# A planned order for one hybrid attention and mLSTM layer: ties between ready steps go to the earliest latest-beginning, taken from a rehearsal of the plan

## The chip, the cores and the metric

The kernel runs on one core of a Trainium2 chip. The metric is device time in microseconds (us) for one execution, the median of several. Engines are named as in the profile: PE (TensorE: matmuls; PEld its weight loads), DVE (VectorE), ACT (ScalarE), POOL (GpSimd) and SP (SyncE, which issues nearly all DMAs here). SPq, ACTq and the like are the queues that issue DMAs.

## What is computed

One encoder layer over 2048 tokens of width 1024, all in float32:

```
xn = rms_norm(x, mix_norm_g)
proj = xn @ w_in                       # q, k, v | mq, mk, mv, mo, i, f | ga, gm
att = chunk_band_attention(aq, ak, av, rel_bias)      # 8 heads of 64, own chunk + 8 before
mqk = silu(causal_depthwise_conv([mq, mk], conv_w, conv_b))
hm = rms_norm(mlstm_chunkwise(mq_c, mk_c, mv, ipre + b_igate, fpre + b_fgate))   # 4 heads of 128
y = sigmoid(ga) * (att @ w_att_proj) + sigmoid(gm) * ((sigmoid(mo) * hm) @ w_mlstm_proj)
x = x + y @ w_out
x = x + square(relu(rms_norm(x, ffn_norm_g) @ w_up)) @ w_down      # 1024 -> 4096 -> 1024
out = rms_norm(x, final_norm_g)
```

## The kernel before

**Arithmetic.** Each float32 operand of a large product is split into a rounded high part and a rest (type fp32r): ACT casts the high part, DVE subtracts to get the rest. A product of two tiles is then three matmuls of 128x128 by 128x512 (high by high, high by rest, rest by high); `pe` steps of the large products hold three such matmuls. The large products use Strassen's scheme with seven sub-products per 2x2 of blocks (`quad`, `product`, `down`): sums of activation blocks (L1765 for the input and output operands, L1855 to L1864 for the up projection's) and of weight blocks (L520, or L438 through DRAM) come ahead of the split, and the products are added into their places by DVE (L1798, L780, L755, L2183) behind it.

**Tiles.** A weight tile of 128x1024 lands in one of 4 `wraw` buffers, is split by L501 (ACT, high) and L503 (DVE, rest) into one of 3 `wsp` buffers, and feeds 24 matmuls. An activation tile of 128x512 is split into one of 28 `r` buffers by L1109 (ACT) and L1114 (DVE), with a scale by L1111 and L1116; `r<-u` are the hidden activations of the feed-forward, read back from DRAM. Products gather in 8 PSUM banks. `ctx`, `tmp` and `sc` are working buffers of 128x512 or somewhat more.

**Stages on PE, from the trace.** Two blocks of v and mv (L562 to L564), from 98 us the other input columns of the first half of the tokens (L631), from 455 us the input columns of the second half (L662 and L667) with the projections of token blocks 0 and 1, from 1097 us the out and up projections of the first half (L631), then its down projection (L562 to L564) with the projections of blocks 2 and 3 (`project`) up to about 2010 us, then out, up and down of the second half, and from 2678 us to 2725 us a last seventh product with tokens on the partitions (L856). Attention (L1337 scores, L1369 transposes of the probabilities, L1262 the weighted sum) and the mLSTM recurrence (L1586 to L1651) run between the large products from 463 to 1936 us. An attention head's result for block 2 goes straight into an operand of `project`: L1275, L1280 (DVE), L1285 (ACT, high part), L1287 (DVE, rest). At the end, for each of four token tiles, L2282 and L2286 (DVE) add and scale, L2298 (ACT) squares and sums, L2289 (DVE) and L2291 (POOL) make the factor, L2308 (ACT) or L2311 (DVE) applies it, and L2316 (ACTq) or L2319 (SPq) stores.

**What sets the order.** Nothing above is written out in its final order. Every piece of work is a generator (a thread) that yields steps: an engine and a modelled duration, or a wait for an event, or a request for buffers of a pool. `Flow.run` is the planner: it keeps a modelled clock per engine, and again and again takes, of all threads whose next step could run, the one with the smallest key

```
key = (start, prio, th.n)
```

where `start` is the later of the engine's clock and the moment that the step's inputs are there (by the model's latencies), `prio` is the thread's fixed priority (weights 0, most evacuations and splits 1, sums of weights 3, the dense products on PE 5; a `!` behind the engine's name puts -1), and `th.n` the order of creation. The step's instructions are then written, so the order of the plan becomes the order of each engine's instructions. Where several steps wait for a busy engine, all have the same `start` (the engine's clock), so `prio` and then `th.n` decide between them. On PE, steps of `prio` below 5 (attention, recurrence) are put off by `FAR` or `SLACK`, 1300 model ns. SP's steps are planned in the same way. A callback (`near`) ties each DVE instruction to those planned 10 us before it, and each ACT instruction to those 6 us before, so that the framework's own scheduler does not move them far.

## Time and profile before

| | |
|---|---|
| median of three runs, lowest, highest | 2738.43, 2737.99, 2741.09 us |
| the profiled execution's own time, its span | 2734.73, 2732.9 us |
| granted TensorE clock | 1.00 |
| busy: DVE, ACT, POOL | 2074.9 us (76%), 1527.6 us (56%), 48.2 us (2%) |
| matmul records, DVE and ACT instructions | 12832, 3685, 2650 |
| HBM, mean | 245 GB/s |
| 16 DMA engines, packets of SP's queue | 73.0% |

Busy times are of one execution, and the span is that of its first to last instruction. "Idle before" of an instruction is the time its engine stood still ahead of it, with the instruction that ended the wait behind an arrow.

### The profile page before, as it was taken

The page shows a single profiled execution, that of the slowest core. Times are in us where ns is not written, and L with a number is a line of the kernel's source. Part 1 is how long each engine was busy: PE and PEld are TensorE (multiplying, and loading weights), DVE is VectorE, ACT ScalarE, POOL GpSimd, SP SyncE. Part 2 cuts the span into 40 slices and gives each one's busy share as a digit, 9 for nine tenths or more (in the row PEclk, how much of TensorE's full clock was granted, in tenths as well). Part 3 has the DMA queues.
Part 4 walks back from the last instruction along what each step waited for, and adds up shares of the span by engine and source line. Part 5 has one row for each costly group of instructions (what it writes and reads, how often), then busy time and mean ns, then how long its engine had stood idle before and what let it go on. Part 6 is the DMA issues. An engine that isn't in the chain of part 4 may idle for free.

```text
span 2732.9 us, 38055 instructions
## 1 busy us (share of the span) xinstructions
PE 2717.4 (99%) x12832; PEld 2262.6 (83%) x12832; DVE 2074.9 (76%) x3685; ACT 1527.6 (56%) x2650; POOL 48.2 (2%) x79
## 2 busy tenths in 40 slices
PE   9999999999999999999999999999999999999998
PEld 8878888888888888888888888888888888888887
DVE  7868776788875778897767798879888665657675
ACT  6545446676742534566556776666445565554443
POOL 0000000000000000000000000000000000000000
PEclk9999999999999999999999999999999999999999
DMA  8877678888868889767768876877774454588863
GB/s 297 280 257 259 243 266 280 269 250 266 281 215 271 306 307 303 239 216 261 254 230 279 277 254 204 255 229 245 252 233 160 154 204 158 185 276 272 286 234 138
DMA packets 331240, 672.53 MB, mean 246 GB/s; under 512 B 36788, under 2 KB 66100, under 8 KB 331044
## 3 DMA queue, kind: packets, MB, share of 16 engines
q1 hardware_dynamic: 330324, 669.03, 73.0%
q8 instruction: 101, 1.65, 0.2%
q10 hardware_dynamic: 720, 1.06, 0.1%
q14 instruction: 95, 0.78, 0.1%
HBM read 458.27 MB, written 211.68 MB: 245 GB/s over the span
## 4 chain that ended last, share of the span: by engine, by line
PE 90%; DVE 6%; issue 1%; DMA 1%; ACT 1%; POOL 0%; SPq 0%; POOLq 0%; DVEq 0%; ACTq 0%
PE bank L631 37%; PE bank L662 11%; PE bank L562 9%; PE bank L563 9%; PE bank L564 9%; PE bank L667 3%; PE bank L1337 2%; PE bank L1262 2%; PE bank L1369 2%; PE bank L856 1%; DVE wsp L503 1%; DVE r L1114 1%; DMA x<-ctx 1%; PE bank L1420 1%; PE bank L1597 1%
## 5 line engine op out<-in xcount | busy, mean ns | idle before, releaser
L631 PE MATMUL bank<-r,wsp 128*128 128x512 f32 x4872 | 1110.6, 390 | 1.9 <-ACT r L1109 1.1
L631 PEld LDWEIGHTS bank<-r,wsp 128*128 128x128 f32 x4872 | 912.6, 188 | 194.9 <-ACT r L1109 1.8
L501 ACT CAST wsp<-wraw 128x1024 fp32r<-128x1024 f32 x439 | 461.3, 1051 | 540.9 <-PE bank L563 203.7
L503 DVE TENSOR_TENSOR wsp<-wraw,wsp 128x1024 fp32r<-128x1024 f32 x439 | 536.1, 1221 | 277.8 <-ACT wsp L501 271.8
L562 PE MATMUL bank<-r,wsp 128*128 128x512 f32 x1088 | 430.4, 396 | 0.0
L563 PE MATMUL bank<-r,wsp 128*128 128x512 f32 x1088 | 425.0, 391 | 1.6 <-DVE r L1287 1.6
L564 PE MATMUL bank<-r,wsp 128*128 128x512 f32 x1088 | 424.7, 390 | 0.0
L662 PE MATMUL bank<-r,wsp 128*128 128x512 f32 x1512 | 368.5, 393 | 1.3 <-DVE ctx L755 0.8
L662 PEld LDWEIGHTS bank<-r,wsp 128*128 128x128 f32 x1512 | 278.9, 188 | 58.3 <-DVE ctx L755 1.5
L564 PEld LDWEIGHTS bank<-r,wsp 128*128 128x128 f32 x1088 | 204.2, 188 | 43.6
L563 PEld LDWEIGHTS bank<-r,wsp 128*128 128x128 f32 x1088 | 204.6, 188 | 40.4 <-DVE r L1287 2.0
L562 PEld LDWEIGHTS bank<-r,wsp 128*128 128x128 f32 x1088 | 204.3, 188 | 38.5 <-DVE r L1374 0.3
L1114 DVE TENSOR_TENSOR r<-r 128x512 fp32r<-128x512 f32 x271 | 179.8, 688 | 16.1 <-ACT r L1109 13.4
L1109 ACT CAST r<-r 128x512 fp32r<-128x512 f32 x271 | 157.9, 617 | 31.0 <-DMA r<-u 27.6
L1798 DVE TENSOR_TENSOR ctx<-bank,ctx 128x512 f32<-128x512 f32 x150 | 103.0, 687 | 64.1 <-PE bank L631 64.0
L520 DVE TENSOR_TENSOR wraw<-wraw,wraw 128x1024 f32<-128x1024 f32 x112 | 136.2, 1219 | 3.8 <-DMA wsum<-wraw 2.8
L1350 ACT ACTIVATE sc<-sc,scs 128x640 f32<-128x640 f32 (+4 forms) x128 | 97.5, 762 | 67.1 <-DVE scs L1343 66.4
L2119 ACT ACTIVATE ctx<-ctx 128x512 f32<-128x512 f32 x96 | 60.5, 630 | 105.7 <-DVE ctx L1798 105.6
L1790 ACT COPY ctx<-bank 128x512 f32<-128x512 f32 x150 | 87.3, 582 | 53.4 <-PE bank L631 51.3
L1374 DVE TENSOR_TENSOR r<-bank,r 128x512 fp32r<-128x512 f32 (+1 forms) x168 | 95.6, 593 | 14.5 <-ACT r L1372 13.8
L1372 ACT CAST r<-bank 128x512 fp32r<-128x512 f32 (+1 forms) x168 | 80.9, 515 | 31.3 <-PE bank L1369 29.3
L1262 PE MATMUL bank<-r,r 128*128 128x512 f32 x336 | 95.2, 365 | 0.0
(257 smaller groups left out, 3060.6 us busy)
## 6 DMA issues: line engine op xcount, KB each, us to landing
wraw<-in_wf SPq DMA_DIRECT2D x196, 512.0 KB, 4.4
r<-u SPq DMA_DIRECT2D x224, 256.0 KB, 4.2
wraw<-wsum SPq DMA_DIRECT2D x104, 512.0 KB, 4.5
u<-ctx SPq DMA_DIRECT2D x128, 256.0 KB, 2.4
u<-tmp SPq DMA_DIRECT2D x96, 256.0 KB, 2.4
wraw<-in_w SPq DMA_DIRECT2D x47, 512.0 KB, 4.4
ctx<-in_wf SPq DMA_DIRECT2D x88, 256.0 KB, 3.9
wsum<-ctx SPq DMA_DIRECT2D x88, 256.0 KB, 3.4
```

The costliest lines, as they stand in the source:

```text
L501: nc.scalar.copy(w[:, 0], raw)
L503: nc.vector.tensor_sub(w[:, 1], raw, w[:, 0].bitcast(F32))
L520: V.tensor_sub(dst, x, y)
L562: mm(ps, lh, rh, start=first, stop=False)
L563: mm(ps, lh, rl, start=False, stop=False)
L564: mm(ps, ll, rh, start=False, stop=last)
L631: mm(ps, wv[:, x, k, n], a[:, y], start=new and k == 0 and x == y == 0, stop=k == 3 and x == 1, skip_group_check=True)
L662: mm(ps, wv[:, x, k, n], a[:, y], start=start and x == y == 0, stop=stop and x == 1, skip_group_check=True)
L1109: self.nc.scalar.copy(dst[:, 0], src)
L1114: self.nc.vector.tensor_sub(dst[:, 1], src, dst[:, 0].bitcast(F32))
L1262: nc.tensor.matmul(bkv[:, :, c0:c0 + w], st, sl[:, :, o:o + w], start=n == 0, stop=n == total - 1)
L1798: nc.vector.tensor_add(t[:, o:o + 512], ps, t[:, o:o + 512])
```

## The change

`kernel` now builds the layer twice. The first time (`Layer(Blank(), ...)`) every tile, DRAM tensor and engine call is a `Blank` that swallows what is done to it, so nothing is written; the planner runs by the old key and logs each step with its start, its end and the steps that it waited for (`th.by`, through events, buffer pools and the thread's own previous step). `dues` then goes through the log backwards and gives each step the latest beginning with which everything behind it would still begin in time; the only fixed points are the dense PE steps (`prio` 5), which must begin when they did in the rehearsal. Steps that lead to none of these get a very late time. The second build plans again, and on ACT, DVE, POOL and SP the second place of the key is now that latest beginning instead of `prio` (steps with `!` keep coming first). The first place of the key, the earliest start, is as before, and on PE the whole key is.

```diff
--- before.py
+++ after.py
@@ -69,14 +69,40 @@
 
 
 
+ENGS = ("act", "dve", "pool", "sp")
+PEDUE = lambda prio: prio == 5
+SPM = 0.0
+TRIES = 1
+
+
 class Event:
     def __init__(self):
         self.at = None
+        self.by = ()
+
+
+class Blank:
+
+
...
+    def tile(self, *a, **kw):
+        return Blank()
 
 
 class Pool:
     def __init__(self, items):
-        self.free = [((0.0, "sp"), n, i) for n, i in enumerate(items)]
+        self.free = [((0.0, "sp"), n, i, ()) for n, i in enumerate(items)]
         self.n = len(items)
 
 
@@ -94,9 +120,10 @@
 
 
 class Thread:
-    def __init__(self, gen, prio, n, at):
+    def __init__(self, gen, prio, n, at, name, by):
         self.gen, self.prio, self.n, self.at = gen, prio, n, at
         self.req = None
+        self.name, self.kids, self.steps, self.by = name, 0, 0, list(by)
 
 
 class Flow:
@@ -114,7 +141,9 @@
                dve=dict(pe=220.0, act=130.0, dve=130.0, pool=155.0), pool=dict(pe=290.0, act=130.0, dve=60.0),
                sp=dict())
 
-    def __init__(self):
+    def __init__(self, due=None):
+        self.due = due
+        self.log, self.cur = [], None
         self.now = (0.0, "sp")
         self.clock = dict(pe=0.0, act=0.0, dve=0.0, pool=0.0, sp=0.0)
         self.ready, self.blocked = [], []
@@ -122,17 +151,24 @@
         self.full = False
 
     def spawn(self, gen, prio=2):
-        th = Thread(gen, prio, self.count, self.now)
+        up = self.cur
+        if up is None:
+            th = Thread(gen, prio, self.count, self.now, f"{self.count}", ())
+        else:
+            th = Thread(gen, prio, self.count, self.now, f"{up.name}.{up.kids}", up.by)
+            up.kids += 1
         self.count += 1
         self._step(th, None)
 
     def set(self, ev):
         ev.at = self.now
+        ev.by = tuple(self.cur.by)
 
     def put(self, pool, *items, late=0.0):
 
         for i in items:
-            pool.free.append(((self.now[0] + late, self.now[1]), pool.n, i))
+            by = tuple((x, y + late) for x, y in self.cur.by) if self.cur else ()
+            pool.free.append(((self.now[0] + late, self.now[1]), pool.n, i, by))
             pool.n += 1
             if isinstance(pool, Banks):
                 pool.dense.discard(id(i))
@@ -143,6 +179,7 @@
             if any(e.at is None for e in r[1]):
                 return False, None
             th.at = max([th.at] + [e.at for e in r[1]])
+            th.by += [x for e in r[1] for x in e.by]
             return True, None
         pool, n = r[1], r[2]
         room = len(pool.free)
@@ -157,19 +194,21 @@
         pool.free.sort(key=lambda x: x[:2])
         got, pool.free = pool.free[:n], pool.free[n:]
         th.at = max([th.at] + [g[0] for g in got])
+        th.by += [x for g in got for x in g[3]]
         if kind == "dense":
             pool.dense.update(id(g[2]) for g in got)
         return True, [g[2] for g in got]
 
     def _step(self, th, value):
-        keep = self.now
+        keep, up = self.now, self.cur
         while True:
-            self.now = max(self.now, th.at)
+            self.now, self.cur = max(self.now, th.at), th
             try:
                 th.req = th.gen.send(value)
             except StopIteration:
-                self.now = keep
+                self.now, self.cur = keep, up
                 return
+            self.cur = up
             if th.req[0] in ("wait", "get", "dense"):
                 ok, value = self._grant(th)
                 if ok:
@@ -212,6 +251,8 @@
                     start = max(self.clock[e], start)
                     if e == "pe" and self.full and not full:
                         start += self.SWITCH
+                    if self.due is not None and e in ENGS:
+                        prio = -1e12 if prio < 0 else self.due.get((th.name, th.steps), 1e12)
                     key = (start, prio, th.n)
                     if best is None or key < best[0]:
                         best = (key, th, e, full)
@@ -223,10 +264,31 @@
             self.clock[e] = end
             if len(th.req) > 2:
                 end += th.req[2]
+            at = th.name, th.steps
+            self.log.append((at, e, start, end, th.prio, {x: y for x, y in sorted(th.by, key=lambda x: x[1])}))
+            th.steps += 1
+            th.by = [(at, 0.0)]
             th.at = self.now = (end, e)
             self._step(th, e)
 
 
+def dues(log):
+    late, of = {}, {x[0]: x[1:4] for x in log}
+    due = {}
+    for at, e, start, end, prio, by in reversed(log):
+        end_by = late.get(at, 1e12) - (SPM if e == "sp" else 0.0)
+        begin = end_by - (end - start)
+        if e == "pe" and PEDUE(prio):
+            begin = min(begin, start)
+        due[at] = begin
+        for x, wait in by.items():
+            lat = Flow.LAT[of[x][0]].get(e, 0.0) + wait
+            if e == "pe" and prio < 5:
+                lat += Flow.FAR
+            late[x] = min(late.get(x, 1e12), begin - lat)
+    return due
+
+
 def act_ns(n, ps=False, ap=0):
     return (51 if ps else 93) + 0.834 * n + 93 * ap
 
@@ -248,9 +310,9 @@
 class Layer:
     LATE, LANDED = 4000.0, 10000.0
 
-    def __init__(self, tc, pool, psum, io):
-        self.tc, self.nc, self.io = tc, tc.nc, io
-        self.fl = Flow()
+    def __init__(self, nc, pool, psum, io, due=None):
+        self.nc, self.io = nc, io
+        self.fl = Flow(due)
         self.make_tiles(pool, psum)
 
 
@@ -1152,13 +1214,17 @@
         both = tile.rearrange("p (a c) -> p a c", a=2)
         for x in range(2):
             yield "sp", 1000, 2000
-            nc.sync.dma_start(both[:, x], bass.AP(self.rbd.ap().tensor, (2 * j + x) * 512, [[1, P], [1, 384]]))
+            nc.sync.dma_start(both[:, x], self.row_at((2 * j + x) * 512))
         yield "pool", 160
         nc.gpsimd.memset(both[0:64, :, 0:64], NEG)
         bias += [both[:, 0], both[:, 1]]
         fl.set(read[2])
         yield "wait", read[:2]
         fl.put(self.bias, tile)
+
+    def row_at(self, o):
+        t = self.rbd.ap().tensor
+        return t if isinstance(t, Blank) else bass.AP(t, o, [[1, P], [1, 384]])
 
     def head(self, b, h, vs, k, q, bias, read):
         fl, nc, B = self.fl, self.nc, self.blk[b]
@@ -2539,7 +2605,12 @@
 
             ahead = {mybir.EngineType.DVE: 10000, mybir.EngineType.Activation: 6000}
             past = {e: collections.deque() for e in ahead}
-            layer = Layer(tc, pool, psum, io)
+            due = None
+            for _ in range(TRIES):
+                empty = Layer(Blank(), Blank(), Blank(), Blank(), due)
+                empty.build()
+                due = dues(empty.fl.log)
+            layer = Layer(nc, pool, psum, io, due)
 
             def near(ins):
                 p = past.get(ins.engine)
```

The instructions themselves stay the same but for 8 scalings of attention probabilities, which the planner may give to either engine and which go from ACT (L1357) to DVE (L1355). The same source line stands 62 to 66 lines lower in the changed file: L503 is L565 there, L1114 is L1176, L1287 is L1353, L1798 is L1864. On PE the sequence of the large products stays the same but for a few dozen neighbours; the other matmuls between them (attention, recurrence) stand earlier, at the median by some 35 to 65 places among the large products' matmuls.

Three places show how instructions move. The first is DVE at the change from the out projection to the up projection of the first half of the tokens (in the trace of before 1184 to 1191 us). `wraw`, `wsp` are weights; L1855 and L1114 make the operands `r26` and `r6` of the second weight tile's product. Before:

```order
L520 TENSOR_TENSOR wraw1_65<-wraw3_67,wraw1_65 128x1024
L1864 TENSOR_TENSOR ctx7_120<-ctx0_113,ctx7_120 128x512
L520 TENSOR_TENSOR wraw0_64<-wraw2_66,wraw0_64 128x1024
L1798 TENSOR_TENSOR ctx6_119<-bank1_130,ctx6_119 128x512
L503 TENSOR_TENSOR wsp1_62<-wraw3_67,wsp1_62 128x1024
L1858 TENSOR_TENSOR tmp3_110<-tmp4_111,ctx11_124 128x512
L1114 TENSOR_TENSOR r26_94<-tmp2_109,r26_94 128x512
L1861 TENSOR_TENSOR tmp0_107<-ctx9_122,tmp3_110 128x512
L1114 TENSOR_TENSOR r6_74<-tmp4_111,r6_74 128x512
```

And with the change, where the same two operands are `r19` and `r6` (L1921 is L1855, L1924 is L1858, L1176 is L1114, L582 is L520, L565 is L503):

```order
L1921 TENSOR_TENSOR tmp5_112<-ctx10_123,ctx2_115 128x512
L1921 TENSOR_TENSOR tmp3_110<-ctx4_117,ctx14_127 128x512
L582 TENSOR_TENSOR wraw0_64<-wraw3_67,wraw0_64 128x1024
L1176 TENSOR_TENSOR r19_87<-tmp5_112,r19_87 128x512
L1176 TENSOR_TENSOR r6_74<-tmp3_110,r6_74 128x512
L1924 TENSOR_TENSOR tmp0_107<-tmp5_112,ctx9_122 128x512
L565 TENSOR_TENSOR wsp0_61<-wraw0_64,wsp0_61 128x1024
L1924 TENSOR_TENSOR tmp2_109<-tmp3_110,ctx7_120 128x512
L1864 TENSOR_TENSOR ctx5_118<-bank7_136,ctx5_118 128x512
L1176 TENSOR_TENSOR r5_73<-tmp0_107,r5_73 128x512
L1176 TENSOR_TENSOR r8_76<-tmp2_109,r8_76 128x512
```

Before, two sums of weights and a weight's split stand ahead of the split of the first operand; with the change one sum does, and the weight's split comes behind both operands.

The second is DVE at the end of attention in token block 2, where the last head's result becomes an operand of `project` (in the trace 1938 to 1945 us). Before:

```order
L1275 TENSOR_TENSOR tmp5_112<-bank0_129,tmp5_112 64x512
L2153 TENSOR_TENSOR tmp2_109<-tmp2_109,tmp3_110 128x512
L1280 TENSOR_TENSOR tmp5_112<-tmp5_112 64x256
L2157 TENSOR_TENSOR ctx10_123<-ctx10_123,tmp2_109 128x512
L2183 TENSOR_TENSOR ctx4_117<-bank7_136,ctx4_117 128x512
L1653 TENSOR_TENSOR ctx11_124<-bank3_132,tmp4_111 128x512
L503 TENSOR_TENSOR wsp0_61<-wraw2_66,wsp0_61 128x1024
L1114 TENSOR_TENSOR r5_73<-ctx11_124,r5_73 128x512
L1287 TENSOR_TENSOR r11_79<-tmp5_112,r11_79 64x256
```

With the change (L1341 is L1275, L1346 is L1280, L1353 is L1287; here the last two units stand together):

```order
L1341 TENSOR_TENSOR tmp3_110<-bank1_130,tmp3_110 64x512
L565 TENSOR_TENSOR wsp2_63<-wraw2_66,wsp2_63 128x1024
L1346 TENSOR_TENSOR tmp3_110<-tmp3_110 64x256
L1341 TENSOR_TENSOR tmp1_108<-bank0_129,tmp1_108 64x512
L1353 TENSOR_TENSOR r1_69<-tmp3_110,r1_69 64x256
L1346 TENSOR_TENSOR tmp1_108<-tmp1_108 64x256
L1353 TENSOR_TENSOR r1_69<-tmp1_108,r1_69 64x256
L1176 TENSOR_TENSOR r19_87<-r19_87 128x512
```

Before, six instructions of other work, among them the residual's L2153 and L2157, stand between the first and the last step of that unit (L1275 and L1287); with the change only the last step of the unit before it does, and the last attention matmul on PE stands 75 places of the large products earlier.

The third is ACT at the end of the program, token tiles 3 and 4 of four. Before:

```order
L2316 DMA out_x<-sc3_105 128x512
L2298 ACTIVATE tmp0_107,r_q_170<-bank5_134 128x512
L2308 ACTIVATE sc0_99<-sc0_99,r_z3_181 128x512
L2308 ACTIVATE ctx3_116<-ctx3_116,r_z3_181 128x512
L2316 DMA out_x<-sc0_99 128x512
L2298 ACTIVATE tmp1_108,r_q_170<-bank7_136 128x512
L2308 ACTIVATE sc1_101<-sc1_101,r_z3_181 128x512
L2316 DMA out_x<-sc1_101 128x512
```

With the change (L2364 is L2298, L2374 is L2308, L2382 is L2316):

```order
L2382 DMA out_x<-sc1_101 128x512
L2364 ACTIVATE tmp5_112,r_q_170<-bank1_130 128x512
L2374 ACTIVATE ctx0_113<-ctx0_113,r_z3_181 128x512
L2364 ACTIVATE tmp2_109,r_q_170<-bank7_136 128x512
L2374 ACTIVATE sc2_103<-sc2_103,r_z3_181 128x512
L2374 ACTIVATE sc3_105<-sc3_105,r_z3_181 128x512
L2382 DMA out_x<-sc2_103 128x512
L2382 DMA out_x<-sc3_105 128x512
```

The square of the fourth tile goes ahead of one scaling of the third, the last scalings stand together, and both last stores from ACT's queue stand behind them. On DVE there, L2282 of the fourth tile moves ahead of L2289 of the third.

8 lines of the change are left out of this document (added).

## The prediction

> **What bounds the kernel now.** I read the page's busy times first, then the chain of work that ended last, PE's table of waits, and busy time by stage.
>
> ```profile
> span 2732.9 us, 38055 instructions
> PE 2717.4 (99%) x12832; PEld 2262.6 (83%) x12832; DVE 2074.9 (76%) x3685; ACT 1527.6 (56%) x2650; POOL 48.2 (2%) x79
> ...
> 261.83 193.16 PE bank L631 x852
> ```
>
> PE is busy for all but 15.5 us of the span. The last row, from the chain, says what its busy time is made of: 852 matmuls of 128x512 in 193.16 us, 226.7 ns each, back to back for as long as nothing is waited for. The change leaves every matmul in place, so this floor stays, and only what is not such work can be won. [...]
>
> ```profile
> 1100.00:1200.00 100.00, 99.19 (x434) 80.77 (x434) 92.30 (x126) 56.81 (x84) 0.00 (x0) 1.00 0.63 208
> 1500.00:2000.00 500.00, 497.70 (x2605) 422.91 (x2604) 424.30 (x980) 320.13 (x652) 17.08 (x29) 1.00 0.77 244
> 2680.00:2733.00 53.00, 45.58 (x217) 37.86 (x216) 25.65 (x40) 18.36 (x31) 4.17 (x5) 0.98 0.31 116
> ```
>
> The columns are the stretch and its length, then busy time of PE, PEld, DVE, ACT, POOL. Of the 15.5 us, 53.00 - 45.58 = 7.4 lie in the tail behind the last product, and 8.1 are spread over the rest. DVE is the fullest helper: 92% and 85% in the first two rows. The waits that make up the 8.1 us are these (total, times, longest):
>
> ```profile
> PE bank L563 <- DVE r L1287: 1.6, 1, 1.6
> PE bank L631 <- ACT r L1109: 1.1, 1, 1.1
> PE bank L1068 <- POOL r_in L1033: 1.0, 1, 1.0
> PE bank L304 <- DVE ones L299: 0.9, 1, 0.9
> PE bank L662 <- DVE ctx L755: 0.8, 1, 0.8
> PE bank L1369 <- ACT sc L1357: 0.6, 2, 0.4
> PE bank L662 <- DVE r L1374: 0.5, 1, 0.5
> PE bank L631 <- DVE r L1114: 0.4, 1, 0.4
> PE bank L1337 <- DVE scs L1343: 0.4, 1, 0.4
> PE bank L631 <- DVE r L1116: 0.3, 1, 0.3
> PE bank L1369 <- DVE scs L1343: 0.2, 1, 0.2
> ```
>
> L304 and L1068 belong to the start, where the change leaves the order nearly as it was. The other nine rows are 5.9 us: all that better-ordered DVE and ACT queues can give back directly.
>
> **The change part by part.** *The wait for L1287, 1.6 us.* This is the end of attention in block 2:
>
> ```profile
> 1938.97 0.69 DVE L1275 TENSOR_TENSOR tmp<-bank,tmp 64x512 f32<-64x512 f32 x1
> 1942.80 1.22 DVE L503 TENSOR_TENSOR wsp<-wraw,wsp 128x1024 fp32r<-128x1024 f32 x1
> 1944.63 0.42 DVE L1287 TENSOR_TENSOR r<-tmp,r 64x256 fp32r<-64x256 f32 x1
> 1945.11 0.50 PE L563 MATMUL bank<-r,wsp 128*128 128x512 f32 x1 [1.58 <-DVE r L1287]
> ```
>
> From L1275 to L1287 go 5.7 us, in which DVE works through other things. In the new order only a step of the unit before it stands among its steps, and attention's last matmul is 75 places earlier, at 226.7 ns some 17 us. That is ten times the wait, so it goes: -1.6 us. The residual's steps, which now come later, feed only additions far ahead of their use.
>
> *The change to the up projection, 0.4 us, and the one before it to the out projection, 0.3 us.*
>
> ```profile
> 1184.42 1.21 DVE L520 TENSOR_TENSOR wraw<-wraw,wraw 128x1024 f32<-128x1024 f32 x1
> 1187.89 1.21 DVE L503 TENSOR_TENSOR wsp<-wraw,wsp 128x1024 fp32r<-128x1024 f32 x1
> 1189.62 0.68 DVE L1114 TENSOR_TENSOR r<-tmp,r 128x512 fp32r<-128x512 f32 x1
> 1190.35 9.89 PE L631 MATMUL bank<-r,wsp 128*128 128x512 f32 x42 [0.44 <-DVE r L1114]
> ```
>
> Two of the three weight instructions ahead of L1114 (1.21 us each) now stand behind it; 2.4 us covers the wait of 0.44: -0.4. Of the L1116 waits at the out projection one of two tight operands stays tight in the new order, so half: -0.15. What pays for it is the weight's split, which comes later; its cover is two weight tiles of 24 matmuls, 24 x 226.7 ns = 5.4 us each, of which it gives up 2.4 at most.
>
> *The wait for L1109, 1.1 us.*
>
> ```profile
> 113.55 0.75 DVE L1705 SCALAR_TENSOR_TENSOR ctx<-ctx,gcol,bias 128x512 f32<-128x512 f32 x1
> 115.73 2.63 PE L631 MATMUL bank<-r,wsp 128*128 128x512 f32 x10 [1.06 <-ACT r L1109]
> ```
>
> DVE feeds this operand late (L1705, then a sum, then ACT's L1109). In the new order one L503 (1.21 us) less stands ahead of it, but small set-up instructions that stood earlier are there now, and the operand is still taken as soon as it is made. Bounds 0 and -1.1; I take -0.5.
>
> *Turns of PE between kinds of matmul.* The float32 transposes and the fp32r products alternate:
>
> ```profile
> 1939.25 0.60 PE L1651 MATMUL bank<-const,ctx 128*128 128x128 f32 x4
> 1939.61 0.48 PE L562 MATMUL bank<-r,wsp 128*128 128x512 f32 x1
> 1939.92 0.40 PE L563 MATMUL bank<-r,wsp 128*128 128x512 f32 x1
> ```
>
> The first product behind transposes takes 0.31 us to the next instead of 0.227: 0.08 us for a turn. In the order of before, PE's stretches of one kind number 413, in the new one 399. If only the turn back costs, 7 x 0.08 = 0.6 us are won, if both do 1.1, if neither is real 0; I take -0.6, since the row shows one direction.
>
> *The tail.* ACT is the queue that ends it:
>
> ```profile
> 2726.74 0.71 ACT L2308 ACTIVATE ctx<-ctx,r_z 128x512 f32<-128x512 f32 x1
> 2727.35 0.57 ACT L2298 ACTIVATE tmp<-bank 128x512 f32<-128x512 f32 x1
> 2728.05 0.16 DVE L2289 SCALAR_TENSOR_TENSOR r_z<-r_q,r_z 128x1 f32<-128x1 f32 x1 [1.01 <-ACT tmp L2298]
> 2728.87 0.72 ACT L2308 ACTIVATE sc<-sc,r_z 128x512 f32<-128x512 f32 x1 [0.85 <-POOL r_z L2291]
> 2729.62 0.34 ACTq L2316 DMA_DIRECT2D out_x<-sc  x1
> ```
>
> With the change DVE makes tile 3's factor behind L2282 of tile 4 (0.70 us), and ACT still wants that factor for one scaling ahead of tile 4's L2298. One scaling (0.71) fewer stands ahead of L2298, 0.70 later is the factor: about even, and the two stores now issue one behind the other, 0.34 us each. Bounds -0.3 and +1.0; +0.4.
>
> *New waits.* Attention stands earlier on PE, which puts its DVE work into a stretch that is 85% full, and the operands of the down projection (L1109, L1114) come closer ahead of their matmuls in two places of the new order. No row of before prices this; the nearest are the waits for the same lines, 0.4 and 1.1 us. Bounds 0 and +2; +0.3, since ACT and DVE gain from the 10 model us that the plan allows each of these loads. The small waits for L755, L1357, L1374 and L1343 (2.5 us together) sit where matmul and evacuation take turns on a bank, with the same neighbours as before: 0, between -1.5 and +1.5.
>
> Sum: -1.6 - 0.4 - 0.15 - 0.5 - 0.6 + 0.4 + 0.3 = -2.55 us. Against the profiled execution's own time (2734.73 us: the span and 1.8 us around it) that gives 2732.2. The median of the timed runs, 2738.43, lies 3.7 above that execution; I carry the difference: **2735.9 us**, with a range of its own from 2733 to 2739.
>
> **The rivals.** *Everything goes* (faster): earliest need first leaves PE no wait behind the start: -5.9, and -1.1 for turns with no loss in the tail, 2731.4 us. For it: the new list gives nearly all operands that were late a longer lead. Against: the waits on banks aren't touched by it.
>
> *It moves nothing that matters*: the earliest start still decides, the latest beginning only breaks ties, and waits stay because the plan's durations aren't the chip's; 2738 us. For it: long runs of DVE's order are the same in both. Against: exactly at the waits for L1287 and L1114 the order does change.
>
> *Weights too late* (slower): weights came first before, now they wait for the need that the plan computes. In the stage with DVE at 92%, the split L503 stands closer ahead of its matmuls: counted in the order in which the planner writes, in places 15 to 33 matmuls lie between its start and the first matmul that needs it (3.4 to 7.5 us at 226.7 ns), where before there were at least 39. If DVE runs more than some 2 us behind its plan there (3.4 less 1.2 for the split itself), PE waits for `wsp`. A price of one L503 (1.21 us) for each weight tile, for half of the 100 / 5.4 = 18 tiles of that stage, is 11 us: 2738.4 - 2.5 + 11 = 2747. For it: an urgent step whose input is late holds up whatever stands behind it; ACT stood 27.6 us behind late operands already:
>
> ```profile
> ACT r L1109 <- DMA r<-u: 27.6, 30, 3.5
> ```
>
> Against: PE lost only 0.7 us in that stage in spite of DVE at 92%, so DVE wasn't 2 us late there. [...]
>
> **How the numbers follow.** A measurement of this kernel tells about 0.2% (5.5 us) from no change. Chances: the sum 0.50, everything goes 0.20, nothing that matters 0.18, weights too late 0.12. The first rival is faster by over 5.5 us, and so is a small part of the sum's own spread (0.06): faster 0.26. Weights too late, and a little of the rest, is slower: 0.14. The remaining 0.60 lies within 0.2%. The range from 2730 to 2743 us leaves out the lower end of the first rival and most of the slower case, under 2 in 10.
>
> **What would show it.** The profile of the changed kernel should have no wait of PE for L1353 (L1287 before) over 0.3 us; no wait for L1176 near 1190 us; PE idle by waits between 3 and 6 us in all, the start's 1.9 among them; PE's busy time 2716 to 2717.5; a tail of 7.4 to 8.4 us behind the last product. The wait for weights would show as PE waiting for L563 or L565, or as several waits of about 1 us between 1100 and 1200 us. A span above 2736 us, or one under 2727, means that the sum is wrong.

## The result and the profile after

| | before | changed |
|---|---|---|
| median of seven runs, lowest, highest | 2737.50, 2734.87, 2741.09 us | 2743.92, 2741.41, 2750.00 us |
| the profiled execution, its span | 2734.73, 2732.9 us | 2748.14, 2746.4 us |
| granted TensorE clock | 1.00 | 0.998 |

The changed kernel takes 1.0029 of the time of before (95% interval 1.0020 to 1.0039), 6.4 us more by the medians. Forecast were 2735.9 us and a range of 2730 to 2743. The profiled execution of the changed kernel lies near the upper end of its seven, that of before just below all of its own, so the two profiles stand 13.4 us apart, twice as far as the medians. That matters below.

Of the lines named below, L693 of the changed kernel is L631 before, L724 is L662, L1171 is L1109, L1173 is L1111, L1178 is L1116, and L2070, which adds a bank to a tile of `ctx`, is L2004. From the page of the changed kernel, the span and the busy times:

```profile
span 2746.4 us, 38046 instructions
PE 2720.0 (99%) x12832; PEld 2264.4 (82%) x12832; DVE 2080.8 (76%) x3693; ACT 1521.4 (55%) x2642; POOL 46.4 (2%) x79
```

Next, PE's table of waits of the changed kernel (total, times, longest), to be read against the eleven rows that the prediction shows of before:

```profile
PE bank L693 <- DVE ctx L2070: 4.5, 1, 4.5
PE bank L693 <- ACT r L1173: 2.0, 1, 2.0
PE bank L1435 <- ACT sc L1423: 1.8, 3, 1.2
PE bank L693 <- DVE ctx L1864: 1.5, 2, 0.9
...
PE bank L1529 <- DVE g_lf L1527: 0.9, 1, 0.9
PE bank L1486 <- DVE ctx L1665: 0.8, 1, 0.8
...
PE bank L1403 <- DVE ctx L1719: 0.7, 1, 0.7
PE bank L1403 <- ACT ctx L1656: 0.6, 1, 0.6
...
PE bank L624 <- ACT wsp L546: 0.6, 1, 0.6
...
PE bank L625 <- DVE wsp L565: 0.5, 1, 0.5
```

The two largest rows of before are gone: no wait for L1353 (1.6 us for L1287 before), none for L1171 (1.1 for L1109). In their place stand one wait of 4.5 us, one of 2.0, and a series of 0.6 to 1.2 us in the softmax and recurrence lines (L1403 to L1529).

**Where the time went.** Both programs put the large matmuls (10560 of them: L562 to L564, L631, L662, L667, L856 before) on PE in the same order, so the k-th of one can be set against the k-th of the other. The table cuts the span at the starts of the 1801st, 3201st, 4101st, 5701st, 7201st, 7701st and 8501st of them; the first stage is counted from PE's first matmul (0.95 us), the tail from the start of the last large one. It gives, in us, how much longer each stage takes than in the profile of before; "other" is what remains, the stages with nothing but large products (and the first 0.95 us). "e12" is a second execution of the changed kernel (below).

| | input columns | attention 1 | out, up 1 | attention 2 | out, up 2 | other | tail | span |
|---|---|---|---|---|---|---|---|---|
| before, us | 432.1 | 451.2 | 366.0 | 495.8 | 181.6 | 798.5 | 7.7 | 2732.9 |
| changed | 0.0 | +3.6 | +2.4 | -0.8 | +7.0 | +0.3 | +0.8 | +13.4 |
| changed, e12 | +1.3 | +4.0 | -0.1 | +0.3 | +0.8 | +0.1 | +0.8 | +7.2 |

In e12 the loss of the out and up projections is nearly gone; that of the first attention stage and of the tail is the same. Of the 3.6 us in the first attention stage 2.6 are more idle time of PE (4.7 us, 2.1 before) and 1.0 is more busy time; in e12 they are 2.8 and 1.2. The same holds for single waits. The three largest of seven rows of PE's waits between 455 and 930 us (4.4 us in all), first in the profiled execution, then in e12:

```profile
PE bank L1435 <- ACT sc L1423: 1.5, 2, 1.2
PE bank L1486 <- DVE ctx L1665: 0.8, 1, 0.8
PE bank L1403 <- ACT ctx L1656: 0.6, 1, 0.6
```
```profile
PE bank L1435 <- ACT sc L1423: 1.5, 2, 1.2
PE bank L1486 <- DVE ctx L1665: 0.8, 1, 0.8
PE bank L1403 <- ACT ctx L1656: 0.6, 1, 0.6
```

So the changed kernel's order makes the waits of the first attention stage, and these return. Those of the out projections need a late transfer as well, and come and go.

**How the 4.5 us came about.** Rows of the changed kernel's timeline, in order of time (engine, line, operation, and in brackets what the engine stood idle for):

```profile
2077.91 0.69 DVE L2070 TENSOR_TENSOR ctx<-bank,ctx 128x512 f32<-128x512 f32 x1 [0.32 <-PE bank L693]
2080.50 0.32 SPq L1781 DMA_DIRECT2D ctx<-x  x1
2083.07 0.72 ACT L1784 ACTIVATE ctx<-ctx,gcol 128x512 f32<-128x512 f32 x1 [4.69 <-DMA ctx<-x]
2083.70 0.60 ACT L1171 CAST r<-ctx 128x512 fp32r<-128x512 f32 x1
2084.33 0.69 DVE L1176 TENSOR_TENSOR r<-ctx,r 128x512 fp32r<-128x512 f32 x1 [5.73 <-ACT r L1171]
2108.75 0.68 DVE L2070 TENSOR_TENSOR ctx<-bank,ctx 128x512 f32<-128x512 f32 x1
2109.57 4.81 PE L693 MATMUL bank<-r,wsp 128*128 128x512 f32 x13 [4.50 <-DVE ctx L2070]
```

Read it from the top. A tile of x is stored and loaded back as an operand of the up projection (L1781); the load is issued at 2080.50, after SP's queue stood 2.7 us for the store that it reads. ACT scales and casts the tile at 2083, and DVE, which reached the step that makes the low half (L1176) at 2078.6, stands idle for 5.73 us: its order has that step next, and nothing else ran on it in that time. DVE has no reserve here: it is busy for 24.1 of the 25 us from 2084 to 2109, and it stays behind until PE lacks a bank, 25 us after the cause. In e12 the same DVE wait is small (two rows of DVE's waits, 2050 to 2110 us; the first is another, of 2.0 us, for a tile of x, of which 0.2 us reached PE):

```profile
DVE ctx L2070 <- DMA ctx<-x: 2.0, 1, 2.0
DVE r L1176 <- ACT r L1171: 1.5, 2, 1.2
```

The 2.0 us have the same form. DVE stood 3.65 us for a late load of `in_xt`. The way from there to PE leads through ACT, whose L1173 then waited 3.0 us in all for sums of DVE (L1831, 1107 to 1118 us), and PE paid twice:

```profile
1107.21 0.69 DVE L2070 TENSOR_TENSOR ctx<-bank,ctx 128x512 f32<-128x512 f32 x1 [3.65 <-DMA ctx<-in_xt]
1113.89 0.73 PE L693 MATMUL bank<-r,wsp 128*128 128x512 f32 x2 [0.54 <-DVE r L1178]
1116.62 4.60 PE L693 MATMUL bank<-r,wsp 128*128 128x512 f32 x12 [2.00 <-ACT r L1173]
```

**A second price.** Behind the 4.50 us come 13 matmuls in 4.81 us; at 226.7 ns they take 2.95. Seven of them start 427 ns apart, and so do seven behind the 2.00 us. The stretches of these two show it in their granted clock, 0.98, the third column from the end (the others as in the prediction):

```profile
1100.00:1200.00 100.00, 97.47 (x422) 79.91 (x422) 89.67 (x123) 56.97 (x84) 0.00 (x0) 0.98 0.62 210
2110.00:2210.00 100.00, 100.00 (x436) 82.58 (x435) 73.23 (x93) 61.00 (x93) 0.00 (x0) 0.98 0.41 148
```

In the 3.4 us from 1116.77 and from 2110.05 us the granted clock is 0.50, on both sides of them 1.00. Each of the two stretches has seven such matmuls: 2 x 7 x 0.2 = 2.8 us. They count as busy: PE's busy time rose by 2.6 us though no matmul was added (in e12, which has no such series, it is 2717.6, as before).

### The profile page after: what moved, and what is told of

Read it like the earlier page. It is cut to its first block, busy times and chain, and to the rows that moved or that the text cites. A ratio compares the mean times of both kernels' runs of the same rounds, so it can differ in the third digit from the quotient of the medians.

```text
span 2746.4 us, 38046 instructions
## 1 busy us (share of the span) xinstructions
PE 2720.0 (99%) x12832; PEld 2264.4 (82%) x12832; DVE 2080.8 (76%) x3693; ACT 1521.4 (55%) x2642; POOL 46.4 (2%) x79
## 4 chain that ended last, share of the span: by engine, by line
PE 72%; DVE 3%; issue 2%; DMA 1%; ACT 1%; POOL 0%; SPq 0%; ACTq 0%; POOLq 0%; DVEq 0%
PE bank L693 25%; PE bank L724 10%; PE bank L626 9%; PE bank L624 9%; PE bank L625 9%; PE bank L729 2%; PE bank L1328 2%; PE bank L1403 2%; PE bank L1435 2%; PE bank L918 1%; DVE wsp L565 1%; PE bank L1678 0%; PE bank L1663 0%; PE bank L1682 0%; ACT wsp L563 0%
## 5 line engine op out<-in xcount | busy, mean ns | idle before, releaser
L693 PE MATMUL bank<-r,wsp 128*128 128x512 f32 x4872 | 1114.3, 390 | 8.7 <-DVE ctx L2070 4.5
L693 PEld LDWEIGHTS bank<-r,wsp 128*128 128x128 f32 x4872 | 915.3, 188 | 202.1 <-issue 5.3
L565 DVE TENSOR_TENSOR wsp<-wraw,wsp 128x1024 fp32r<-128x1024 f32 x439 | 536.3, 1222 | 256.1 <-ACT wsp L563 247.3
L724 PE MATMUL bank<-r,wsp 128*128 128x512 f32 x1512 | 366.1, 393 | 0.0
L724 PEld LDWEIGHTS bank<-r,wsp 128*128 128x128 f32 x1512 | 279.5, 188 | 54.8 <-issue 0.2
L1176 DVE TENSOR_TENSOR r<-r 128x512 fp32r<-128x512 f32 x271 | 179.2, 685 | 25.7 <-ACT r L1171 24.6
L1171 ACT CAST r<-r 128x512 fp32r<-128x512 f32 x271 | 157.9, 617 | 43.3 <-DMA r<-u 38.4
L1864 DVE TENSOR_TENSOR ctx<-bank,ctx 128x512 f32<-128x512 f32 x150 | 102.9, 687 | 70.9 <-PE bank L693 69.2
L582 DVE TENSOR_TENSOR wraw<-wraw,wraw 128x1024 f32<-128x1024 f32 x112 | 136.4, 1219 | 1.3 <-DMA wsum<-wraw 0.3
L1403 PE MATMUL bank<-r,r 128*128 128x256 f32 (+2 forms) x464 | 89.5, 311 | 1.4 <-DVE ctx L1719 0.7
```

What stands on the lines that cost most here:

```text
L565: nc.vector.tensor_sub(w[:, 1], raw, w[:, 0].bitcast(F32))
L582: V.tensor_sub(dst, x, y)
L693: mm(ps, wv[:, x, k, n], a[:, y], start=new and k == 0 and x == y == 0, stop=k == 3 and x == 1, skip_group_check=True)
L724: mm(ps, wv[:, x, k, n], a[:, y], start=start and x == y == 0, stop=stop and x == 1, skip_group_check=True)
L1171: self.nc.scalar.copy(dst[:, 0], src)
L1176: self.nc.vector.tensor_sub(dst[:, 1], src, dst[:, 0].bitcast(F32))
```

## The experiments

All are timed against the kernel before on the same chip. Their stages, as in the table above (one profile each, against the one profile of before; a `*` marks a stage in which the new order does not decide on ACT and DVE):

| | attention 1 | out, up 1 | attention 2 | out, up 2 | tail | span | ratio, 95% interval |
|---|---|---|---|---|---|---|---|
| e1 SP by priority | +1.4 | -2.1 | +5.4 | +1.2 | +0.8 | +5.6 | 1.0016 (1.0007 to 1.0025) |
| e2 only SP | +11.5* | +2.4* | +0.6* | +0.9* | 0.0* | +16.5 | 1.0052 (1.0038 to 1.0066) |
| e3 only DVE | +6.3 | -1.9 | +10.3 | +0.2 | +0.5 | +17.2 | 1.0047 (1.0035 to 1.0060) |
| e4 margin 2 us | +6.6 | +2.4 | +1.3 | +1.7 | +0.8 | +11.5 | 1.0046 (1.0033 to 1.0058) |
| e5 loads first | +5.0 | +2.7 | -0.3 | +2.9 | +0.8 | +12.2 | 1.0037 (1.0024 to 1.0050) |
| e6 all PE steps fixed, SP by priority | +5.1 | -2.0 | -1.1 | +0.3 | +1.0 | +2.3 | 0.9995 (0.9986 to 1.0004) |
| e7 before, FAR 1310 | +0.7* | +1.2* | +0.1* | +0.3* | 0.0* | +4.1 | 0.9998 (0.9989 to 1.0007) |
| e8 before, SWITCH 86 | -0.1* | +1.9* | +0.4* | +0.1* | 0.0* | +4.8 | 1.0007 (0.9998 to 1.0015) |
| e9 as e6, not in attention 1 | +2.7* | -0.8 | -1.3 | +0.7 | +0.1* | 0.0 | 0.9978 (0.9969 to 0.9988) |
| e18 the kernel of e9 again | -0.3* | -2.4 | -1.1 | +0.6 | +0.1* | -4.7 | 0.9982 (0.9973 to 0.9991) |
| e10 as e9, not in attention 2 | +1.8* | -0.9 | +1.5* | +1.2 | 0.0* | +1.9 | 0.9993 (0.9984 to 1.0002) |
| e11 in attention 1 alone | +5.9 | 0.0* | +0.9* | +0.5* | 0.0* | +7.6 | 1.0010 (1.0002 to 1.0019) |
| e16 as e11, DVE alone | +5.4 | +1.9* | 0.0* | +1.0* | 0.0* | +7.8 | 1.0018 (1.0009 to 1.0027) |
| e13 as e11, reserve 2600 | -0.9 | +1.6* | +36.9* | +0.8* | 0.0* | +39.9 | 1.0130 (1.0116 to 1.0143) |
| e14 before, reserve 2600 | +2.9* | -0.8* | +38.3* | +0.1* | +0.1* | +41.3 | 1.0147 (1.0133 to 1.0160) |
| e15 as e9, with SP | +13.1* | -0.1 | -0.3 | +6.0 | -0.1* | +17.5 | 1.0047 (1.0034 to 1.0060) |
| e17 as e6, reserve 2600 in attention 1 | -1.0 | -2.2 | -0.5 | +0.5 | +0.1* | -4.0 | 0.9977 (0.9967 to 0.9987) |

How far one stage of one profile can be trusted is in the table itself: e9 and e18 are one kernel, and differ by 3.0 us in the first attention stage and by 1.6 in the first out and up projections. Nearly all of the 3.0 us is one wait of PE, 1.93 us for L818 in e9 and 0.4 in e18, with eight matmuls at 427 ns behind the longer one. And e7 and e8, whose ratios are 1.000, have spans 4 to 5 us above the profile of before, since that execution lies at the lower end of its kind. So a single entry under about 3 us is no finding.

### Which engine's order: e1, e2, e3, e4

The theories at this point: the loads come too late because of SP's order (LOADS), DVE's and ACT's order leaves no reserve (HELPERS), or the loss is attention's (ATTENTION).

**e1.** SP by the fixed priority.

```diff
-ENGS = ("act", "dve", "pool", "sp")
+ENGS = ("act", "dve", "pool")
```

> ACT, DVE and POOL by the latest beginning as in the changed kernel, SP by the fixed priority as before. Theory LOADS (SP now issues the loads of in_xt, yp and x near their latest beginning; they land late, DVE stands 3.65 us at 1103.6 and 5.73 us at 2078.6 in order behind one late operand, and PE pays 4.5 and 2.0 us some microseconds later): both long waits of PE go, and the slower matmuls behind them; from the changed kernel's 2746.4 us of span come off 4.5 + 2.0 + 0.5 + about 3, so 2736 us, ratio to before 0.998 to 1.000. Theory HELPERS (the order of DVE and ACT itself leaves a nearly full DVE no reserve): the long waits, or others like them in the out projections, stay; ratio 1.002 to 1.004. Theory ATTENTION (the losses between 455 and 930 us, 3.6 us): these 3.6 us stay in both cases.

Measured 1.0016, 2741.62 us, between the two forecasts. The long waits in the out and up projections went, as LOADS said, and the first of these stages is quicker than before; but the second attention stage lost 5.4 us. ATTENTION's 3.6 us did not stay: the first attention stage lost 1.4, and PE's waits there (455 to 930 us) come to 2.0 us, as before (1.9), where the changed kernel has 4.4:

```profile
PE bank L1328 <- DVE r L1440: 1.5, 2, 0.8
PE bank L724 <- DVE scs L1409: 0.3, 1, 0.3
PE bank L1435 <- DVE sc L1421: 0.2, 1, 0.2
```

So the changed kernel's waits in that stage need SP's new order too, as far as one profile can tell.

**e2.** SP alone in the new order.

```diff
-ENGS = ("act", "dve", "pool", "sp")
+ENGS = ("sp",)
```

> Only SP by the latest beginning, ACT, DVE and POOL by the fixed priority as before. LOADS: the loads are late here too; one or two waits of PE of 2 us or more in an out projection, ratio 1.001 to 1.004. HELPERS: no loss, ratio 0.999 to 1.001. ATTENTION: the stretch from 455 to 930 us takes as long as before within 1 us.

Measured 1.0052: dearer than the whole change. There is a wait of 2.60 us for L2070 in the first up projection, as LOADS has it. But most of the loss, 11.5 us, lies in the first attention stage, where ATTENTION forecast at most 1 us.

**e3.** DVE alone.

```diff
-ENGS = ("act", "dve", "pool", "sp")
+ENGS = ("dve",)
```

> Only DVE by the latest beginning. LOADS: no long wait in the out projections, ratio 0.998 to 1.000, and the wait behind attention at 1945 us (1.6 us) is gone as in the changed kernel, since it was DVE's order that removed it. HELPERS: a wait of 2 us or more in an out projection, ratio 1.001 to 1.004.

Measured 1.0047, and neither picture: the out projections are clean and the wait behind attention (1.6 us) is gone, as LOADS said, but 6.3 and 10.3 us are lost in the two attention stages.

**e4.** More distance for SP.

```diff
-SPM = 0.0
+SPM = 2000.0
```

> The changed kernel with the latest beginning of every SP step moved 2000 model ns ahead (and so of all that a store waits for; a store and its reload count twice). LOADS, if the plan prices a load too cheaply (800 + 2000 model ns, where the page shows 4.0 to 4.3 us from issue to landing): the long waits shrink below 1 us, DVE no longer stands over 1.5 us for in_xt or x in the out projections, ratio 0.998 to 1.001. LOADS, if it is the order on the queue (loads stand behind stores that wait) and not the price: as the changed kernel, 1.002 to 1.004. HELPERS: as the changed kernel, 1.002 to 1.004.

Measured 1.0046, so the price of a load in the plan is not what is wrong. The waits for L2070 shrank to 1.1 and 0.8 us, but the out and up projections are no quicker than before (+2.4 and +1.7), and the first attention stage is slower.

### Is it those loads, attention's due times, or any other order: e5, e6, e7, e8

**e5.** Three kinds of transfer go ahead of what else is ready on SP. PE's planned order stays as it is.

```diff
-        ..., [B["x2"] for B in self.blk[2 * s:]], "sp", self.gcol[:, 1])
+        ..., [B["x2"] for B in self.blk[2 * s:]], "sp!", self.gcol[:, 1])
...
-                    yield "sp", 800, 2000
+                    yield "sp!", 800, 2000
                     nc.sync.dma_start(x[:, :512], self.io["xt"][2 * s + h, 4 * hi + 2 * q + n])
...
-        fl.spawn(self.store(self.x2d[2 * s + h].ap()[j], x5, kept), 1)
+        fl.spawn(self.store(self.x2d[2 * s + h].ap()[j], x5, kept, queue="sp!"), 1)
```

> The changed kernel, with the loads of in_xt and of x and the store of x put ahead of other ready steps on SP; the planned order of PE is the changed kernel's to the last matmul. LOADS: the stages of the out and up projections (1068 to 1433 us, and 2043 to about 2230) lose their waits for L2070 and L1173; of the 2.4 and 7.0 us that they lost, at least 7 us come back, and with the gain for L1114 and L1116 they are at or below before's time; span 2737 to 2739, ratio 1.000 to 1.002, the stages of attention as in the changed kernel. If it is not these loads but SP's order elsewhere or the DVE itself: the waits for L2070 stay, 1.002 to 1.004.

Measured 1.0037, so LOADS fails in this narrow form: the waits for L2070 stayed, 2.7 us. A higher rank alone did not free them. SP's waits between 1085 and 1120 us in e5 begin with a load of `in_xt` that stands until the store of `mfar` ahead has freed its buffer:

```profile
SPq L2057 <- DMA mfar<-ctx: 6.5, 5, 3.8
```

**e6.** SP by priority, and attention's PE steps are fixed points too.

```diff
-ENGS = ("act", "dve", "pool", "sp")
-PEDUE = lambda prio: prio == 5
+ENGS = ("act", "dve", "pool")
+PEDUE = lambda prio: True
```

> SP by the fixed priority, and every PE step, attention's and the recurrence's too, is a fixed point of the backward pass, not the dense ones alone. Theory SLACK (without a fixed point of their own, softmax and recurrence steps get a late latest-beginning and wait behind everything on DVE and ACT): the two stages of attention lose the 1.4 and 5.4 us that they lost with SP by priority; ratio 0.997 to 0.999. Theory RESHUFFLE (before's order is a good one among many that differ little, and any other order of DVE and ACT brings a few new waits of 0.5 to 2 us in the stages of attention, where PE, DVE and ACT take turns): these stages still lose 3 to 10 us together, ratio 1.001 to 1.004.

Measured 0.9995, between SLACK and RESHUFFLE: the second attention stage no longer loses, the first does (+5.1).

**e7 and e8.** The kernel before, with one constant of its planner altered by about 1%.

```diff
-    SLACK, FAR = 1300.0, 1300.0
+    SLACK, FAR = 1310.0, 1310.0
```

> The kernel before, without the change, its planner's FAR and SLACK 1310 model ns in place of 1300: no rule is altered, but 839 of 3687 DVE instructions and 349 of ACT's stand in another place. RESHUFFLE: the stages of attention lose 2 to 8 us in new small waits, ratio 1.001 to 1.004. SLACK or LOADS alone: nothing of what costs time in the changed kernel is in here, 0.999 to 1.001.

```diff
-    SWITCH = 85.0
+    SWITCH = 86.0
```

> The kernel before, its planner's cost of a turn of PE 86 model ns in place of 85: 453 of 3687 DVE instructions and 264 of ACT's stand in another place. RESHUFFLE: as for FAR 1310, a smaller loss perhaps, ratio 1.0005 to 1.004. SLACK or LOADS alone: 0.999 to 1.001.

Measured 0.9998 and 1.0007, with the attention stages within 0.7 us of before. RESHUFFLE falls for such small changes: hundreds of instructions may change places at no cost that shows. It is not ruled out for larger ones. In the first attention stage e8 leaves every matmul of attention and recurrence at its place among the large products, e7 moves 496 of 944 and none at the median, while the changed kernel moves 912, at the median 33 large matmuls earlier. An arbitrary order as far from before's was not tried.

### The first attention stage by itself: e9, e10, e11, e16, and the repeat e12

In these the latest beginning decides only in stretches of the planner's time; elsewhere the fixed priority does. SP keeps its priorities, and all PE steps are fixed points, as in e6.

**e9.** Everywhere but in the first attention stage and the tail.

```diff
+SPANS = ((0, 470e3), (900e3, 2740e3))
...
-                    if self.due is not None and e in ENGS:
+                    if self.due is not None and e in ENGS and any(x <= start < y for x, y in SPANS):
```

> SP by the fixed priority; ACT, DVE and POOL by the latest beginning (every PE step a fixed point), but not in the first stage of attention (470 to 900 us of the plan) and not in the tail, where the fixed priority decides as before. LOADS (SP's order cost the two long waits) and a loss in the first attention stage that belongs to the new order inside it: that stage costs at most 1 us more than before (e6: 5.05), the stages ahead of it and of the out and up projections keep e6's gains of 1.7 and 2.0 us, the tail loses nothing; span about 2729 us, ratio 0.997 to 0.999. If the first attention stage's loss comes from elsewhere (what stands ready at its beginning): it still loses 3 to 6 us, ratio 0.999 to 1.001.

Measured 0.9978: 6.3 us faster than before (2732.67 against 2738.98 us). The first attention stage lost 2.7 us in this profile, where at most 1 was forecast, by the wait of 1.93 us named above; in e18 it lost nothing.

**e10.** Not in the second attention stage either.

```diff
-SPANS = ((0, 470e3), (900e3, 2740e3))
+SPANS = ((0, 470e3), (900e3, 1510e3), (2010e3, 2740e3))
```

> As the run before, and the fixed priority in the second stage of attention too (1510 to 2010 us of the plan). If the latest beginning helps there (e6: 1.15 us less than before): 1 us more than that run; if it hurts there (e1: 5.4 us more than before): less than that run. Ratio 0.997 to 1.000.

Measured 0.9993, 5.2 us above e9 where about 1 was forecast: with SP's old order and all PE steps fixed, the new order helps in the second attention stage.

**e11.** The first attention stage alone.

```diff
-SPANS = ((0, 470e3), (900e3, 2740e3))
+SPANS = ((470e3, 900e3),)
```

> The complement: the latest beginning on ACT, DVE and POOL in the first stage of attention alone. A loss that belongs to the new order inside this stage: 3 to 6 us there and nothing elsewhere, ratio 1.001 to 1.0025. If it comes from elsewhere: within 1 us of before in that stage, ratio 0.9993 to 1.0007.

Measured 1.0010, with +5.9 us in that stage and under 1 us in each other. The five largest of seven rows of PE's waits between 455 and 930 us in e11 (lines one further down than in the changed kernel):

```profile
PE bank L1664 <- DMA r<-mfar: 1.2, 1, 1.2
PE bank L730 <- DVE scs L1410: 1.2, 1, 1.2
PE bank L1679 <- DVE ctx L1666: 1.1, 1, 1.1
PE bank L1329 <- DMA r<-vspill: 0.8, 1, 0.8
PE bank L1329 <- DVE ctx L1720: 0.7, 1, 0.7
```

No row is large, and no line stands out. Before, the same stretch had three rows of 1.9 us together (for L755, L1357 and L1374). In e11 the wait behind the second attention stage is back as well, so the new order outside the first stage had removed it:

```profile
PE bank L626 <- DVE r L1354: 1.6, 1, 1.6
```

**e16.** As e11, with DVE alone.

```diff
-ENGS = ("act", "dve", "pool")
+ENGS = ("dve",)
```

> As e11, with DVE alone by the latest beginning in the first stage of attention, ACT and POOL by the fixed priority. OWN ORDER of DVE: 3 to 6 us lost in that stage, ratio 1.001 to 1.0025. If it takes ACT's order as well: within 1.5 us of before there, ratio 0.9995 to 1.0005.

Measured 1.0018, +5.4 us in the stage: with all PE steps as fixed points, DVE's new order alone is enough for the loss. It also changes PE's planned order there (attention 30 large matmuls earlier at the median), so the run doesn't tell DVE's own order from PE's.

**e12.** The changed kernel once more.

> The changed kernel once more, for a second profile. LOADS: the long waits of PE for L2070 near 2105 us and for L1173 near 1115 us come back, each over 1.5 us, with DVE standing over 3 us for one late operand 5 to 30 us ahead of them. If they were a chance of that one execution: at least one of them is under 0.5 us, and its stage loses less than 1 us.

Measured 2741.95 us. The 4.5 us are 0.2, the 2.0 us are 0.9, and another wait, 2.9 us for L1864 in the input columns, is new. So the second forecast holds for the long waits: they belonged to that execution, though not to any order. A wait of 1 us or more for L2070 is in five of the six profiles with SP's new order (the changed kernel, e2, e4, e5 and e15, but not e12) and in none of the fourteen without it.

### Reserve, and SP on top of the best: e13, e14, e15, e17, e18

On PE the planner puts attention's and the recurrence's steps off behind their inputs by 1300 model ns.

**e13 and e14.** Twice this reserve, on e11 and on the kernel before.

```diff
-    SLACK, FAR = 1300.0, 1300.0
+    SLACK, FAR = 2600.0, 2600.0
```

> As e11 (the latest beginning on ACT, DVE and POOL in the first stage of attention alone), and the planner puts off each step of attention and recurrence on PE by 2600 model ns behind its inputs in place of 1300. Theory RESERVE (these steps now stand so close behind DVE and ACT that a delay of 0.5 to 1.2 us reaches PE): the stage's loss of 5.9 us against before shrinks to under 2 us, PE's waits there from 6.3 us to under 3; ratio to before 0.999 to 1.000. Theory OWN ORDER (DVE and ACT do in that stage what is not needed yet, and are late by more than any such reserve): 4 us or more are still lost, ratio 1.001 to 1.002.

> The control: the kernel before with 2600 model ns in place of 1300, fixed priorities throughout. RESERVE: PE's waits in the stages of attention are few already (2.1 and 2.3 us), so at most 2 us to win: 0.999 to 1.0005. OWN ORDER says the same. If the longer reserve itself costs (attention ends later, its buffers come free later): over 1.001, and e13 is then read against this run.

Measured 1.0130 and 1.0147. The control shows why the total says nothing: in the second attention stage the longer reserve costs 37 to 38 us in both, with waits such as this in e14 (1460 to 2000 us):

```profile
PE bank L1369 <- ACT sc L1357: 7.9, 2, 5.0
```

What makes it so dear there was not followed up. In the first stage e13 is 6.8 us better than e11, as RESERVE says, while the same reserve gives the old order nothing (+2.9). In both, attention stands some 110 large matmuls later on PE than before at the median, where e11 has it 27 earlier.

**e17.** As e6, with the longer reserve in the first attention stage alone, and the tail by priority.

```diff
+SPANS = ((0, 2740e3),)
+far = lambda t: 2600.0 if 470e3 <= t < 900e3 else 1300.0
...
-                        start += self.FAR if not full else self.NEAR if self.full else self.SLACK
+                        start += far(t) if not full else self.NEAR if self.full else far(t)
...
-                lat += Flow.FAR
+                lat += far(begin)
```

> SP by the fixed priority, ACT, DVE and POOL by the latest beginning everywhere but in the tail, and in the first stage of attention (470 to 900 us of the plan) a reserve of 2600 model ns in place of 1300 on PE. RESERVE: the first attention stage costs 1 us less than before to 1 us more (e13: 0.9 less; e6 with 1300: 5.05 more), the second stays at e6's 1 us less, ratio 0.996 to 0.998, at or below e9. OWN ORDER or a later price of the delay (as in the second stage with e13 and e14): a loss of 3 us or more in the first stage or behind it, ratio over 0.999.

Measured 0.9977. The first attention stage takes 1.0 us less than before, where e6 took 5.1 more. These are all of PE's waits between 455 and 930 us (two lines further down than in the changed kernel):

```profile
PE bank L1437 <- ACT sc L1425: 1.4, 3, 0.9
PE bank L1330 <- DVE scs L1411: 0.4, 1, 0.4
PE bank L726 <- DVE ctx L819: 0.3, 1, 0.3
```

**e15.** SP's new order on e9.

```diff
-ENGS = ("act", "dve", "pool")
+ENGS = ("act", "dve", "pool", "sp")
```

> As e9 (ratio 0.9978), with SP by the latest beginning too, outside the first stage of attention. LOADS: long waits of PE for L2070, L1864 or L1173 (here L2071, L1865, L1174) of 1 us or more in the out and up projections, in some executions; the median 2 to 6 us above e9, ratio 0.9985 to 1.000. If SP's order costs nothing in the median and only the profiled execution was unlucky: 0.997 to 0.9985.

Measured 1.0047 where e9 has 0.9978: SP's new order costs 17 us on top of the best version (19 by the ratios, since the two ran on different chips), far more than LOADS said. 6.0 us are in the second out and up projections, by a wait of the same form as in the changed kernel (ACT stood 5.2 us for a tile of x, DVE 5.1 us for ACT):

```profile
2115.05 7.31 PE L694 MATMUL bank<-r,wsp 128*128 128x512 f32 x24 [3.89 <-DVE ctx L2071]
```

13.1 us are in the first attention stage, though SP's rule is off inside it; 11.6 of them show between the 2001st and the 2101st large matmul, where attention begins. Part of that is work that has moved there (144 other matmuls against 122 before); PE is idle for 4.7 us instead of 0.2, and its granted clock is 0.66 from 510 to 520 us. SP's order ahead of the stage changes the plan inside it: attention stands 41.5 large matmuls earlier on PE at the median, where e9 leaves every one at its place. What in SP's order does this was not followed up.

**e18.** The kernel of e9 again.

> The kernel of e9 once more. If its gain is one of order and not of one chip: ratio 0.997 to 0.999, PE's waits in the first attention stage under 4 us, none of 1.5 us or more in the second out and up projections.

Measured 0.9982, 2731.08 us: the gain of e9 returns, and PE's waits keep within what was forecast. By the medians e9, e17 and e18 beat the kernel before by about 6 us, and the changed kernel by 11 to 13.

## Why the prediction was wrong

**What it had right.** The waits that it named did go: L1353, L1171 and L1176 are in no table of PE's waits, neither of the changed kernel nor of e12. In the four runs e1, e6, e17 and e18, without long waits there, the first out and up projections take 2.0 to 2.4 us less (forecast 0.55), and the input columns 1.2 to 2.0 less (forecast 0.5); e9, the kernel of e18, has 0.8 and 1.6. Each is below what one profile can place, but they agree. The tail lost 0.8 us (forecast 0.4, bounds -0.3 and +1.0). The floor held: in the stages of large products alone both kernels agree to 0.1 us except for one 0.3.

**The step that failed: "New waits ... Bounds 0 and +2; +0.3", with the small waits put at 0 because they stand "with the same neighbours as before".** The prediction looked for new waits where DVE is 85% full, which is the stretch from 1500 to 2000 us, and at the down projection, and priced them by two waits of the dense products (0.4 and 1.1 us). The second attention stage, which lies there, lost nothing (-0.8 and +0.3). The loss came in the first attention stage, 3.6 and 4.0 us in two executions. Three of the four small waits put at 0 lie in that stage, and the neighbours were not the same: 912 of the 944 matmuls of attention and recurrence stand elsewhere among the large ones. PE's waits there add up to 4.4 us against 1.9 before, none of them over 1.2; the other 1 us is longer busy time.

**Why that stage loses is only in part shown.** The new order inside it is enough (e11, DVE alone in e16), and without it there, and with SP's old order, the loss is gone (e18). But it isn't DVE's alone: SP by itself loses 11.5 us there (e2), and the changed kernel without SP's new order 1.4 (e1). In that stage every softmax step goes PE, DVE, ACT, DVE, PE, and each return to PE is a place where a little lateness can show. The second attention stage has the same hand-overs, though, and lost 5.4 and 10.3 us in e1 and e3 but nothing in the changed kernel and e6. Thin reserve on PE is one explanation: e13 and e17, with twice the reserve, had the loss gone. The other is PE's own planned order, which each of these runs alters as well. Here is how many large matmuls later (minus: earlier) attention and recurrence stand than before, at the median of the first stage, beside what the stage lost:

| | e18 | e1 | e6, e11 | e16 | changed | e2 | e15 | e3 | e13, e17 |
|---|---|---|---|---|---|---|---|---|---|
| place on PE | 0 | -24 | -27 | -30 | -33 | -39 | -41.5 | -45 | +111 |
| loss, us | -0.3 | 1.4 | 5.1, 5.9 | 5.4 | 3.6 | 11.5 | 13.1 | 6.3 | -0.9, -1.0 |

Every run that lost 3 us or more in that stage has it earlier by 27 places or more. In the second stage earlier is not dearer: 75 places and -0.8 us in the changed kernel, 18 places and +5.4 in e1. A kernel with the order of the other engines kept and only PE's order altered was not tried.

**The rival "Weights too late" had the mechanism and not the place.** That "an urgent step whose input is late holds up whatever stands behind it" is what the timeline shows, but for the reloaded tiles of x and for `in_xt` (DVE stood 5.73 and 3.65 us). The weights themselves were on time: PE's waits for `wsp` are 0.6 and 0.5 us, both ahead of 13 us and so outside the stage that was named. The prediction worked out prices for DVE and ACT and gave SP half a sentence: "ACT and DVE gain from the 10 model us that the plan allows each of these loads". By e2 and e15, SP's new order costs 14 to 17 us, most of it in the first attention stage. For the out and up projections a likely reason, argued and not shown, is that a latest beginning is worked out from the plan's latency, while on SP's queue in the changed kernel the reload of x stood 2.7 us for its store, and the load of `in_xt` behind it went out only at 2080.86. Adding 2000 ns (e4) or ranking the loads first (e5) did not remove these waits.

**The argument against that rival was read too broadly.** "PE lost only 0.7 us in that stage in spite of DVE at 92%, so DVE wasn't 2 us late there" was true of the old SP order. It says that this order kept DVE fed, not that DVE has room.

**The turns** (-0.6) did not show. The changes between large and other matmuls fell from 274 to 260 in the first attention stage and from 388 to 362 in the second, but PE's busy time in the two together rose by 0.5 us (1.3 in e12).

**Which part costs what, by the medians.** With SP's order taken back the changed kernel goes from 1.0029 to 1.0016 (e1; the two intervals overlap); e15 against e9 gives SP much more. With attention's PE steps as fixed points besides it is 0.9995 (e6), and with the old order in the first attention stage and the tail 0.9978 (e9). So with these fixed points the rule is worth some 6 us on ACT, DVE and POOL outside that stage; the change as made, which also gives SP the new order and lacks the fixed points, stands 11 to 13 us above that.

## What to carry to other kernels

An order by latest beginning paid here on the compute engines outside the first attention stage, and cost on the queue that issues the DMAs and in that stage; change one engine and one stage at a time. Before a new order is priced by the waits that it removes, see which instructions get new neighbours on the engine that is full, and don't put their waits at nothing because they were short before. A plan's order on one engine changes the others' too, so compare all of them. And profile twice: of the 13.4 us between the first two profiles, some 9 belonged to waits in the out and up projections that the next execution nearly didn't have.
